# A two-layer diffusion block: first norm and projections in program order on three engines, the context's modulation sums queued behind the latents' steps, scalings on ScalarE

## The chip, the cores and the metric

The kernel runs on one core of one Trainium2 chip. The metric is the device time of one execution in microseconds (us). The core has five engines that work at the same time, each on its own queue of instructions in a fixed order: TensorE (PE, matmuls; PEld is its weight load), VectorE (DVE), ScalarE (ACT), GpSimd (POOL) and SyncE (SP, which here only issues DMA transfers; ACT issues a few too). Engines wait for one another through semaphores.

## The reference

512 latent tokens and 256 context tokens of width 1024 go through two layers. Cut to what matters:

```python
for l in range(2):
    sh1, sc1, gt1, sh2, sc2, gt2 = adaln(c, w_mod[l], b_mod[l])             # silu(c) @ w_mod + b_mod, six parts
    csh1, csc1, cgt1, csh2, csc2, cgt2 = adaln(c_ctx, w_mod[l], b_mod[l])   # the same for the context
    h_ctx = rms_norm(ctx, norm1[l]) * (1 + csc1) + csh1
    h = rms_norm(x, norm1[l]) * (1 + sc1) + sh1
    a_b, a_c, a_x, q, k, v, u, sv, g = split(h @ w_in[l])     # q and k: RMS norm per head, then rotary
    attn = softmax(q @ [k, k_ctx].T / 8) @ [v, v_ctx]         # latents see latents and context
    y_a = (a_b * conv3(a_c * a_x)) @ w_a                      # branch A
    y_b = attn @ w_b                                          # branch B
    y_c = (gelu(u) * (w_s @ rms_norm(gelu(sv)) + b_s)) @ w_c  # branch C
    x = x + gt1 * ((sigmoid(g_a) * y_a + sigmoid(g_b) * y_b + sigmoid(g_c) * y_c) @ w_o)
    x = x + gt2 * (silu(h2 @ w_ff1) * (h2 @ w_ff3)) @ w_ff2
    # in layer 0 the context goes through the same; in layer 1 only its keys and values are needed
```

## The kernel before

Everything is fp32, held transposed: channels on the 128 partitions in 8 blocks (KD), tokens along the row; columns 0 to 511 are latents (XS), 512 to 767 context (CS). A product in fp32 is made of three matmuls: each operand is split into a high part, rounded on ACT (L224), and a low part, the difference, on POOL or DVE (L225). `mm` runs high by high, high by low, low by high (L234). Weights arrive in pieces of 128x512 or 128x384 (`ws`, five buffers, L218) and become `wh` and `wl` (four buffers each).

The modulation is not a matmul: for each of the 8 blocks of a section (shift or scale) `mod_sums` loads a 128x1024 tile of w_mod (512 KB, L153) and makes one fused multiply and row sum on DVE (L156) with the activated condition, `sbc[:, 0]` for the latents and `sbc[:, 1]` for the context; `mod_rest` adds the bias and the norm's gain (L165, L168). `wm_stage` gives the tile one of three buffers.

The first layer starts so. x arrives in three transfers; `norm_stats` squares its blocks on ACT (L348, L351), adds them on DVE (L352), sums over partitions on PE (L355), takes the power -0.5 on POOL (L359) and spreads the result over a PSUM bank (RB, L365). Then, for block k = 0 to 7: two modulation sums (scale, then shift), `norm_apply` (y on DVE L374, shift on ACT L376 or L379, split into the pair h[k]; for odd k the low part is L377 on DVE, for even k L225 on POOL), and the six projections of this block (key, value, four queries), which gather in six PSUM banks over all k (`six`). `post_k`, `post_v` and `post_q` take them out: squares on ACT (L436), per-head sums on PE (L440), the gain (L477, L515) and rotary, for which ACT issues DMAs that swap rows (L530), splits (L491 to L494, L519 to L522). Branches A (`branch_a`, the convolution is L605 to L610) and C (`branch_c`, gelu L636, gain L655) project the latents' h again, ten projections with weights of two 256 KB pieces each. After that come the context's norm, keys, values and branch C, and attention.

The order on each queue is made by a planner: it goes through the written order and, by a timing model of its own, lets what is ready sooner go first. Written order gives only the priority. `ctx_mods` writes the context's sums in turns with the branches' steps; the context's norm is written behind them. A few transfers are held back by a one-column copy on POOL into their target (L553, L557, L563, L623).

## Time and profile before

| | us |
|---|---|
| median of 3 runs (1976.04 to 1977.44) | 1976.17 |
| profiled execution, its own time | 1975.22 |
| span of its profile | 1973.4 |
| PE busy | 1879.8 (95%) |
| DVE busy | 1164.6 (59%) |
| ACT busy | 747.8 (38%) |
| POOL busy | 859.9 (44%) |

Times in the profile count from the span's start. Busy shares are averages over the whole span, and stages differ. A row of windows gives, for one stretch, the busy time of each engine with its instructions in brackets, the clock that PE was granted as a share of its 2.4 GHz, the mean busy share of the DMA engines, and what they moved. A wait is put down to what ended it. An instruction's time holds what it waits for once it has started.

### The profile page before, as it was taken

How to read it: one execution, taken by the hardware profiler on the slowest of the kernel's cores; microseconds unless marked ns; L12 is line 12 of the kernel's file. 1: busy time of each engine (PE TensorE's matmuls, PEld its weight loads, DVE VectorE, ACT ScalarE, POOL GpSimd, SP SyncE). 2: the span in 40 equal slices, each digit the busy share in tenths (PEclk: the TensorE clock that was granted, in tenths of full speed). 3: DMA queues.
4: the chain of work that ended last, by engine and by line, in shares of the span. 5: the costliest groups of instructions: out<-in, count | busy, mean ns of one | idle time of the engine just before them, and what ended most of it. 6: DMA issues, size and time to landing. Idle time of an engine off the chain costs nothing.

```text
span 1973.4 us, 27588 instructions
## 1 busy us (share of the span) xinstructions
PE 1879.8 (95%) x10150; PEld 1654.6 (84%) x10150; DVE 1164.6 (59%) x1936; ACT 747.8 (38%) x1459; POOL 859.9 (44%) x722
## 2 busy tenths in 40 slices
PE   5789999999999899999999998999999999999999
PEld 3578998888889789899999987888888888888887
DVE  7877865535359887877676867549523362322222
ACT  4346765222223623232322345448533352313121
POOL 4678743534334415152433347854333253424232
PEclk9989999999999899999999998999999999999999
DMA  8933201324255142323323354410322433332311
GB/s 280 306 101 97 76 27 39 134 76 149 75 185 195 38 144 91 129 91 118 119 95 134 119 183 153 135 34 5 107 90 92 147 108 127 100 102 86 111 43 66
DMA packets 107735, 222.42 MB, mean 113 GB/s; under 512 B 12368, under 2 KB 19792, under 8 KB 107600
## 3 DMA queue, kind: packets, MB, share of 16 engines
q1 hardware_dynamic: 105536, 217.51, 33.0%
q10 hardware_dynamic: 2064, 3.15, 0.6%
q8 instruction: 80, 1.31, 0.3%
q14 instruction: 55, 0.45, 0.1%
HBM read 212.74 MB, written 5.24 MB: 110 GB/s over the span
## 4 chain that ended last, share of the span: by engine, by line
PE 73%; DVE 14%; issue 4%; ACT 3%; DMA 3%; POOL 2%; ACTq 0%; SPq 0%; DVEq 0%; POOLq 0%
PE wide L234 33%; PE pD L234 21%; PE pD L311 5%; PE wide L311 5%; PE pF L234 3%; DMA wm<-in_w_modT 2%; DVE wm L156 2%; PE pO L765 2%; DVE wl L225 2%; PE pPT L759 1%; PE wide L733 1%; DVE junk L156 1%; DVE nm L737 1%; DVE nacc L352 1%; DVE ptl L762 1%
## 5 line engine op out<-in xcount | busy, mean ns | idle before, releaser
L225 POOL TENSOR_TENSOR wl<-ws,wh 128x512 fp32r<-128x512 f32 (+2 forms) x338 | 484.4, 1445 | 462.5 <-ACT wh L224 376.0
L234 PE MATMUL wide<-A,wh 128*128 128x512 f32 (+2 forms) x1728 | 469.3, 367 | 17.4 <-ACT A L224 8.2
L234 PEld LDWEIGHTS wide<-A,wh 128*128 128x128 f32 x1728 | 302.8, 192 | 72.7 <-ACT A L224 10.2
L224 ACT CAST wh<-ws 128x512 fp32r<-128x512 f32 (+2 forms) x536 | 302.2, 607 | 65.4 <-issue 17.5
L234 PE MATMUL wide<-A,wl 128*128 128x512 f32 (+2 forms) x864 | 289.1, 366 | 4.9 <-POOL wl L225 4.9
L225 DVE TENSOR_TENSOR wl<-ws,wh 128x512 fp32r<-128x512 f32 (+1 forms) x198 | 168.4, 851 | 131.5 <-ACT wh L224 121.5
L234 PE MATMUL pD<-A,wh 128*128 128x512 f32 (+1 forms) x784 | 238.2, 384 | 6.6 <-ACT A L224 2.8
L156 DVE SCALAR_TENSOR_TENSOR wm<-wm,fixed 128x1024 f32<-128x1024 f32 x112 | 152.1, 1361 | 49.4 <-DMA wm<-in_w_modT 47.5
L234 PEld LDWEIGHTS wide<-A,wl 128*128 128x128 f32 x864 | 154.2, 192 | 30.7 <-POOL wl L225 6.3
L234 PEld LDWEIGHTS pD<-A,wh 128*128 128x128 f32 x784 | 147.3, 193 | 35.0 <-ACT A L224 3.2
L234 PE MATMUL wide<-u,wh 128*128 128x512 f32 (+1 forms) x600 | 149.5, 352 | 0.9 <-DVE xr L990 0.9
L234 PE MATMUL pD<-A,wl 128*128 128x512 f32 (+1 forms) x392 | 148.7, 382 | 0.0
L234 PE MATMUL pD<-u,wh 128*128 128x512 f32 (+1 forms) x456 | 118.2, 357 | 0.0
L234 PEld LDWEIGHTS wide<-u,wh 128*128 128x128 f32 x600 | 98.9, 188 | 17.3 <-DVE xr L990 1.2
L742 POOL TENSOR_SCALAR pp<-pp,nm 128x768 f32<-128x768 f32 (+1 forms) x80 | 66.8, 836 | 101.2 <-DVE nm L741 65.5
L225 POOL TENSOR_TENSOR u<-su,u 128x768 fp32r<-128x768 f32 (+1 forms) x44 | 72.4, 1655 | 85.2 <-ACT u L224 85.2
L803 ACT ACTIVATE gate<-wide 128x512 f32<-128x512 f32 (+1 forms) x56 | 26.7, 516 | 199.8 <-PE wide L234 199.2
L156 DVE SCALAR_TENSOR_TENSOR junk<-wm,fixed 128x1024 f32<-128x1024 f32 x48 | 68.2, 1420 | 54.3 <-DMA wm<-in_w_modT 47.2
L809 DVE SCALAR_TENSOR_TENSOR gate<-gate,pD 128x512 f32<-128x512 f32 (+1 forms) x45 | 25.6, 596 | 122.4 <-PE pD L234 99.8
L224 ACT CAST wh<-fw 128x512 fp32r<-128x512 f32 x80 | 48.5, 615 | 121.8 <-DVE fw L263 106.3
L224 ACT CAST u<-su 128x768 fp32r<-128x768 f32 (+1 forms) x44 | 31.7, 728 | 165.7 <-DVE su L885 93.9
L234 PE MATMUL wide<-u,wl 128*128 128x512 f32 (+1 forms) x300 | 89.4, 351 | 0.0
(248 smaller groups left out, 3827.0 us busy)
## 6 DMA issues: line engine op xcount, KB each, us to landing
ws<-in_w SPq DMA_DIRECT2D x252, 256.0 KB, 3.8
wm<-in_w_modT SPq DMA_DIRECT2D x112, 512.0 KB, 4.3
ws<-in_w_in SPq DMA_DIRECT2D x184, 256.0 KB, 2.9
ws<-in_w_o SPq DMA_DIRECT2D x48, 256.0 KB, 5.4
ws<-in_w_abc SPq DMA_DIRECT2D x32, 256.0 KB, 2.7
ws<-in_w_six SPq DMA_DIRECT2D x16, 192.0 KB, 4.5
xr<-in_xT SPq DMA_DIRECT2D x8, 384.0 KB, 7.6
ws<-in_w SPq DMA_DIRECT2D x16, 192.0 KB, 2.4
```

Of the source, the lines that this page charges most:

```text
L156: nc.vector.scalar_tensor_tensor(o, t, 1.0, sbc[:, c, :], op0=ALU.mult, op1=ALU.mult, accum_out=MOD[l][:, sec, b, c:c + 1])
L224: nc.scalar.copy(hi, src)
L225: (lo_eng or nc.gpsimd).tensor_tensor(lo, src, f(hi), op=ALU.subtract)
L234: nc.tensor.matmul(d[:, :b - a], lhsT=ww, rhs=aa[:, a:b], start=kk == 0 and i == 0, stop=kk == n - 1 and i == 2)
L311: nc.tensor.matmul(D, lhsT=x[:, kk * P:(kk + 1) * P], rhs=a, start=kk == 0 and i == 0, stop=kk == 3 and i == 2)
L352: nc.vector.tensor_tensor(acc[:, :n], acc[:, :n], sq[:, :n], op=ALU.add)
L733: nc.tensor.matmul(D[:, a - k0:b - k0], lhsT=q[:, c * P - q0:(c + 1) * P - q0], rhs=kt[:, a:b], start=i == 0, stop=i == 1)
L737: nc.vector.tensor_reduce(nm[:, 0:1], D[:, :nk], axis=AX.X, op=ALU.max, negate=True)
L742: nc.gpsimd.tensor_scalar(pt[:, :nk], pt[:, :nk], nm[:, 3:4], 0.0, op0=ALU.mult, op1=ALU.add)
L765: nc.tensor.matmul(o[:, 0:256], lhsT=v3[:, kt, :], rhs=pp[:, j * 256:(j + 1) * 256], start=gi == 0 and j == 0 and i == 0, stop=gi == len(k ...
L803: nc.scalar.activation(g_[:, a:e], D, AF.Tanh, scale=0.5)
L809: nc.vector.scalar_tensor_tensor(g_[:, a:e], g_[:, a:e], 1.0, D, op0=ALU.add, op1=ALU.mult)
```

## The change

The first norm and the six projections stand in a block in which DVE, POOL and ACT issue in the written order; PE and SP, and what is written outside the block, stay with the planner. The written order is new: the sums for block k + 1 stand around the step of block k (the scale's sum inside `norm_apply`, between y and the shift, the shift's sum behind it), and the weights of block k + 1 are split ahead of the matmuls of block k. The first scale sum stands between the squares' additions and the statistics. Latents' and context's first-section loads have a tag of their own, `wm0`, with five buffers. The Silu of the condition stands behind the squares, and a one-column Silu at the start loads its table.

The context's sums, and then its norm, are written step by step in turn with the branches (`ctx_norm`), each step within `later(...)`: what it issues on DVE (for the norm, on ACT too) comes in that engine's queue behind the latents' step marked last (`mark` on DVE, `amark` on ACT). That is an order of issue, not a wait for its end. Five kinds of scalings by a per-channel factor move from DVE (`tensor_scalar`) to ACT (`activation` with Copy and a scale): key, queries, the convolution's middle tap, the gain in branch C, for latents and context and in both layers. The context's x comes in one 1 MB transfer instead of eight, behind one copy.

```diff
-    def norm_stats(X, a, b):
+    def norm_stats(X, a, b, then=None):
...
+        if then:
+            then()
         st = pst("st")
...
         nc.vector.scalar_tensor_tensor(y, X[k][:, a:b], g, RB[:, :n], op0=ALU.mult, op1=ALU.mult)
+        if between:
+            between()
...
+    scr = sm.tile([P, 1], F32, tag="scr", name="scr", bufs=2)
+    nc.scalar.activation(scr, half[:, 0:1], AF.Silu)
...
-    nc.scalar.activation(sbc[:, 0, :], sbc[:, 0, :], AF.Silu)
+    mark, amark = [None], [None]
+
+    def later(ins):
+
+        return tc.issue_after(ins.ins)
...
-            nc.vector.tensor_scalar(kk[:, :n], D, vcol(l, V_KG), None, op0=ALU.mult)
+            nc.scalar.activation(kk[:, :n], D, AF.Copy, scale=vcol(l, V_KG))
...
-                nc.vector.tensor_scalar(qq[:, :n], D, vcol(l, V_QG), None, op0=ALU.mult)
+                nc.scalar.activation(qq[:, :n], D, AF.Copy, scale=vcol(l, V_QG))
...
-                nc.vector.tensor_tensor(qb[0:64, :n], qq[64:128, :n], f(qb[64:128, :n]), op=ALU.subtract)
+                mark[0] = nc.vector.tensor_tensor(qb[0:64, :n], qq[64:128, :n], f(qb[64:128, :n]), op=ALU.subtract)
...
-            RB = norm_stats(X, *XS)
-            for k in range(KD):
-                for sec in (1, 0):
-                    mod_sums(0, sec, k, (0,), wm_stage())
-                    mod_rest(0, sec, k, 1, 0, 1)
-                norm_apply(X, RB, G1[0], MOD[0][:, 0], k, *XS, h[k])
-                for hb in range(2):
-                    w = load_piece(w_six[k][:, hb * 384:(hb + 1) * 384])
-                    for b in range(3):
-                        mm([six[3 * hb + b]], w[b:b + 1], h, [XS], k=k)
...
-            for k in range(KD):
-                nc.gpsimd.tensor_copy(X[k][:, SEQ:SEQ + 1], f(h[4][0][:, 0:1]))
-                nc.sync.dma_start(X[k][:, SEQ:NT], xT[k][:, SEQ:NT])
+            def first_sums(k, secs):
+                if k < KD:
+                    for sec in secs:
+                        mod_sums(0, sec, k, (0,), wp.tile([P, 1024], F32, tag="wm0", name="wm0", bufs=5))
+                        mod_rest(0, sec, k, 1, 0, 1)
+
+            def six_weights(k):
+                return [p for hb in range(2) for p in load_piece(w_six[k][:, hb * 384:(hb + 1) * 384])]
+
+            with tc.manual_schedule(engines={mybir.EngineType.DVE, mybir.EngineType.Pool, mybir.EngineType.Activation}):
+                RB = norm_stats(X, *XS, lambda: (nc.scalar.activation(sbc[:, 0, :], sbc[:, 0, :], AF.Silu),
+                                                 first_sums(0, (1,))))
+                first_sums(0, (0,))
+                w = six_weights(0)
+                for k in range(KD):
+                    norm_apply(X, RB, G1[0], MOD[0][:, 0], k, *XS, h[k], lambda: first_sums(k + 1, (1,)))
+                    first_sums(k + 1, (0,))
+                    wk, w = w, six_weights(k + 1) if k < KD - 1 else None
+                    for b in range(6):
+                        mm([six[b]], wk[b:b + 1], h, [XS], k=k)
+                    if k == 0:
+                        nc.gpsimd.tensor_copy(sbc[:, 1, 0:1], f(h[0][0][:, 0:1]))
+                        nc.sync.dma_start(sbc[:, 1, :], conds[1:2, :].to_broadcast([P, 1024]))
+                    if k == 6:
+                        nc.scalar.activation(sbc[:, 1, :], sbc[:, 1, :], AF.Silu)
+            nc.gpsimd.tensor_copy(xin[:, :, SEQ:SEQ + 1], f(h[4][0][:, None, 0:1]).to_broadcast([P, KD, 1]))
+            nc.sync.dma_start(xin[:, :, SEQ:NT], xT[:, :, SEQ:NT].rearrange("k p t -> p k t"))
...
-                    nc.vector.tensor_scalar(cv[:, :n], z[:, :n], cw[1], None, op0=ALU.mult)
+                    nc.scalar.activation(cv[:, :n], z[:, :n], AF.Copy, scale=cw[1])
...
-                nc.vector.tensor_scalar(gs[t][:, :n], gs[t][:, :n], vcol(l, V_SG + t), None, op0=ALU.mult)
+                nc.scalar.activation(gs[t][:, :n], gs[t][:, :n], AF.Copy, scale=vcol(l, V_SG + t))
...
-            def ctx_mods():
+            def ctx_norm():
                 for k in range(KD):
-                    for sec in (1, 0):
-                        mod_sums(0, sec, k, (1,), wm_stage())
-                        if k == KD - 1:
-                            mod_rest(0, sec, 0, KD, 1, 1)
+                    with later(mark[0]):
+                        for sec in (1, 0):
+                            mod_sums(0, sec, k, (1,), wp.tile([P, 1024], F32, tag="wm0", name="wm0", bufs=5))
+                            if k == KD - 1:
+                                mod_rest(0, sec, 0, KD, 1, 1)
+                    yield
+                rest = norm(X, G1[0], MOD[0][:, 0], *CS, h)
+                go = True
+                while go:
+                    with later(mark[0]), later(amark[0]):
+                        go = next(rest, rest) is not rest
                     yield
...
-            run(ctx_mods(), small_x())
-            for _ in norm(X, G1[0], MOD[0][:, 0], *CS, h):
-                pass
+            run(small_x(), ctx_norm())
```

Left out of the diff here: `mark[0] =` or `amark[0] =` stands also before the convolution branch's copy (L595), its first product (L599) and its last (L610), before gelu (L636) and before the sum of branch C's squares (L646).

## Rows read from the trace of the kernel before

**Rows 1.** Windows of 100 us: length, PE, PEld, DVE, ACT, POOL (instructions), clock, DMA share, GB/s.
```profile
0.00:100.00 100.00, 62.39 (x259) 49.56 (x260) 80.38 (x132) 37.49 (x67) 56.80 (x51) 0.95 0.87 292
100.00:200.00 100.00, 90.54 (x528) 79.25 (x527) 73.25 (x121) 55.52 (x111) 74.75 (x60) 0.93 0.32 98
200.00:300.00 100.00, 98.72 (x719) 92.42 (x719) 79.31 (x157) 70.69 (x142) 59.42 (x56) 1.00 0.18 53
...
1200.00:1300.00 100.00, 99.98 (x504) 84.61 (x503) 56.33 (x78) 47.24 (x88) 75.84 (x55) 1.00 0.34 109
```

**Rows 2.** Windows cut at the stage's own events, the same columns.
```profile
27.00:64.00 37.00, 33.05 (x129) 25.28 (x130) 33.93 (x59) 16.41 (x34) 27.23 (x30) 1.00 0.86 289
64.00:90.00 26.00, 22.02 (x104) 18.13 (x103) 22.50 (x28) 8.74 (x16) 22.09 (x12) 0.99 0.88 299
90.00:107.00 17.00, 10.84 (x36) 8.55 (x36) 15.22 (x28) 2.79 (x5) 4.41 (x3) 0.61 0.73 231
107.00:142.00 35.00, 29.91 (x128) 24.15 (x129) 26.39 (x28) 16.54 (x29) 26.90 (x18) 0.90 0.27 83
142.00:166.00 24.00, 22.13 (x133) 19.95 (x131) 17.30 (x31) 11.20 (x24) 14.95 (x14) 0.93 0.26 81
```

**Rows 3.** PE's waits, 64 to 166 us: waiter, releaser, total, times, longest.
```profile
PE pKB L483 <- DVE v L507: 6.1, 1, 6.1
```

**Rows 4.** Instructions by line and shape, 64 to 166 or 0 to 166 us.
```profile
L156 DVE SCALAR_TENSOR_TENSOR wm<-wm,fixed 128x1024 f32<-128x1024 f32 x16 | 24.9, 1575 | 4.4 <-DMA wm<-in_w_modT 4.3
...
L352 DVE TENSOR_TENSOR nacc<-nacc,nsq 128x256 f32<-128x256 f32 x7 | 5.7, 807 | 0.5 <-ACT nsq L351 0.3
...
L655 DVE TENSOR_SCALAR gel<-gel,fixed 128x512 f32<-128x512 f32 x2 | 3.1, 1540 | 2.7 <-ACT gsq L644 2.7
...
L515 DVE TENSOR_SCALAR qq<-pD,fixed 128x512 f32<-128x512 f32 x2 | 1.5, 744 | 0.0
...
L436 ACT ACTIVATE hsq<-wide 128x512 f32<-128x512 f32 x3 | 1.8, 599 | 9.3 <-DMA sw<-kk 7.4 <-POOL wl L225 1.6 <-PE phst L440 0.3
```

**Rows 5.** Timeline of DVE, 57 to 170 us: start, duration, instruction.
```profile
63.04 0.75 DVE L377 SCALAR_TENSOR_TENSOR A<-ny,fixed,A 128x512 fp32r<-128x512 f32 x1
...
82.00 0.47 DVE L605 TENSOR_SCALAR acv<-az,fixed 128x512 f32<-128x512 f32 x1
...
102.10 1.23 DVE L156 SCALAR_TENSOR_TENSOR wm<-wm,fixed 128x1024 f32<-128x1024 f32 x1
...
126.44 1.35 DVE L605 TENSOR_SCALAR acv<-az,fixed 128x512 f32<-128x512 f32 x1
...
139.98 1.66 DVE L522 TENSOR_TENSOR qb<-qq,qb 64x512 fp32r<-64x512 f32 x1
...
163.86 0.63 DVE L377 SCALAR_TENSOR_TENSOR A<-ny,fixed,A 128x256 fp32r<-128x256 f32 x1
```

**Rows 6.** Timeline of all engines, 0 to 42 us.
```profile
17.36 1.22 DVE L156 SCALAR_TENSOR_TENSOR wm<-wm,fixed 128x1024 f32<-128x1024 f32 x1
...
24.88 1.40 DVE L374 SCALAR_TENSOR_TENSOR ny<-xin,fixed,pRB 128x512 f32<-128x512 f32 x2
```

**Rows 7.** Chain of work that ended last, 13 to 70 us: start, duration, what.
```profile
42.48 5.54 DMA wm<-in_w_modT
```

**Rows 8.** The DMA queue's own waits (SP), 60 to 170 us.
```profile
SPq L153 <- DVE wm L156: 11.7, 7, 2.7
```

**Rows 9.** Timelines of DVE and of POOL around 27 us.
```profile
26.27 1.21 DVE L156 SCALAR_TENSOR_TENSOR wm<-wm,fixed 128x1024 f32<-128x1024 f32 x1
...
27.41 2.28 DVE L156 SCALAR_TENSOR_TENSOR wm<-wm,fixed 128x1024 f32<-128x1024 f32 x1
...
27.10 1.51 POOL L225 TENSOR_TENSOR A<-ny,A 128x512 fp32r<-128x512 f32 x1 [3.24 <-ACT A L224]
```

**Rows 10.** POOL's instructions by line and shape, 64 to 166 us.
```profile
L225 POOL TENSOR_TENSOR wl<-ws,wh 128x512 fp32r<-128x512 f32 x26 | 42.5, 1648 | 4.6 <-ACT wh L224 4.4
...
L225 POOL TENSOR_TENSOR B<-mx,B 128x512 fp32r<-128x512 f32 x1 | 1.3, 1288 | 1.6 <-ACT B L224 1.6
```

More of the change, by code (lines that the diff above doesn't have):

```diff
@@ L366, in norm_stats, with norm_apply @@
         return RB
-    def norm_apply(X, RB, G, S, k, a, b, hk):
+    def norm_apply(X, RB, G, S, k, a, b, hk, between=None):
         n = b - a
@@ L553, in dit_block @@
-            nc.gpsimd.tensor_copy(sbc[:, 1, 0:1], f(h[0][0][:, 0:1]))
-            nc.sync.dma_start(sbc[:, 1, :], conds[1:2, :].to_broadcast([P, 1024]))
-            nc.scalar.activation(sbc[:, 1, :], sbc[:, 1, :], AF.Silu)
-            for k in range(KD):
-                nc.gpsimd.tensor_copy(X[k][:, SEQ:SEQ + 1], f(h[4][0][:, 0:1]))
-                nc.sync.dma_start(X[k][:, SEQ:NT], xT[k][:, SEQ:NT])
+            def first_sums(k, secs):
[3 more added lines that the diff above has]
+                        mod_rest(0, sec, k, 1, 0, 1)
@@ L594, in ev_ac @@
                     ACV["c"] = slot("ac", n)
-                    nc.scalar.copy(ACV["c"][:, :n], D)
+                    amark[0] = nc.scalar.copy(ACV["c"][:, :n], D)
                 def ev_ax(D, *_):
                     ACV["z"] = slot("az", n)
-                    nc.vector.tensor_tensor(ACV["z"][:, :n], ACV["c"][:, :n], D, op=ALU.mult)
+                    mark[0] = nc.vector.tensor_tensor(ACV["z"][:, :n], ACV["c"][:, :n], D, op=ALU.mult)
                 def ev_ab(D, *_):
@@ L609, in ev_ab @@
                                                    op0=ALU.mult, op1=ALU.add)
-                    nc.vector.tensor_tensor(cv[:, :n], cv[:, :n], D, op=ALU.mult)
+                    mark[0] = nc.vector.tensor_tensor(cv[:, :n], cv[:, :n], D, op=ALU.mult)
                     if ("a", t) not in br:
@@ L635, in go @@
                     g_ = slot("gel", n)
-                    nc.scalar.activation(g_[:, :n], D, AF.Gelu_apprx_tanh)
+                    amark[0] = nc.scalar.activation(g_[:, :n], D, AF.Gelu_apprx_tanh)
                     lst.append(g_)
@@ L645, in branch_c @@
             nc.scalar.activation(sq1[:, :n], gs[1][:, :n], AF.Square)
-            nc.vector.tensor_tensor(sq0[:, :n], sq0[:, :n], sq1[:, :n], op=ALU.add)
+            mark[0] = nc.vector.tensor_tensor(sq0[:, :n], sq0[:, :n], sq1[:, :n], op=ALU.add)
             st = pst("gst")
```

## The prediction

> **What bounds the kernel now.** I read windows of 100 us first: TensorE (PE) is busy 62.4 us of the first hundred, 90.5 of the second, 98.7 of the third and 99.98 of the hundred from 1200 us, where the second layer's projections run [rows 1]. So what can be won lies ahead of 200 us, and the reader is to see there a kernel that is not yet limited by PE. Windows cut at the stage's own events tell why [rows 2]. From 27 to 64 us (first norm, six projections) VectorE (DVE) is busy 33.9 of 37 us and the DMA engines 86%. From 64 to 90 DVE is busy 22.5 of 26 us, GpSimd (POOL) 22.1. From 90 to 107 DVE has 15.2 of 17 us, but PE 10.8 us at a mean granted clock of 0.61, and POOL 4.4: both wait for DVE. The longest PE wait in the stage says for what [rows 3]: 6.1 us ahead of the transposes for the keys (L483), until DVE had split the values (L507). From 107 to 142 and 142 to 166 DVE falls to 26.4 of 35 and 17.3 of 24 us.
>
> What filled DVE early? By line, 16 sums of L156 take 24.9 us between 64 and 166 us [rows 4]; they are the context's, and they are issued ahead of keys and queries that PE was waiting for. In DVE's timeline four events mark the stage [rows 5]: the last piece of the latents' h is made at 63.0 (done 63.8), the last of the context's sums starts at 102.1, the last query's low half ends at 139.98 + 1.66 = 141.6, and the context's norm ends at 163.86 + 0.63 = 164.5. Only then do context keys, context values and with them the scores have their input. I price the change by these dates: what the context's norm gains, the end gains, since behind it PE is busy 98.7 of 100 us [rows 1].
>
> **The start.** Between the squares and the statistics DVE did three sums (the last of them stands in [rows 6]), and the first normalized block came at 24.88 us. In the new order one sum stands there. Two sums of 1.22 us go: 2.4 us, the first block at about 22.5. The Silu that moves behind the squares, and the table load ahead of them, I cost at nothing: x arrives underneath. Without that cover it is one more step on ScalarE (ACT), below twice the 0.60 us of half as many columns [rows 4].
>
> **First norm to last h piece.** It takes 63.8 - 24.9 = 38.9 us now. In it the chain shows a wait of 5.54 us for one modulation load [rows 7]; and DVE adds the context's squares there (L352 at 256 columns, seven for 5.7 us [rows 4]). In the new order the context's norm is behind, five buffers instead of three take the loads, and SP's waits for them (11.7 us in seven, [rows 8], partly later) should shrink. What remains is DVE's own step: per block two sums, y and, every other time, a low half: 2 x 1.3 + 0.74 + 0.37 + 0.4 of small steps = 4.1 us, 33 us for eight. Against that stand in-order stalls on three engines: DVE, POOL and ACT can no longer step past a late load. So 0 to 6 us are won (6 is 38.9 - 33); I take 2.6, a little under the middle because of the stalls, and the last h piece ends at 63.8 - 2.4 - 2.6 = 58.8 us. The eight gated context loads become one behind one POOL copy; seven POOL copies go, under 1.1 us on an engine with gaps: nothing.
>
> **From h to the last query.** DVE's busy time from 64 to 142 is 22.5 + 15.2 + 26.4 = 64.1 us [rows 2]. The 16 sums (24.9 us) leave it. So do the scalings: key and four queries, each like the 744 ns row of L515, 3.7 us; two of L605, 1.8 us; the first of the two L655, 1.5 us [rows 4]. A part of the last two is waiting for POOL (L605 took 0.47 us at 82.0 and 1.35 at 126.4, [rows 5]), so I count 5.6, not 7. That leaves 33.6 us. How fully will DVE be busy without the sums as filler? The nearest row is 107 to 142 us, when no sum was left: 26.4 of 35, 75%. So 33.6 / 0.75 = 44.8 us, and the last query ends at 58.8 + 44.8 = 103.6 us; at full occupation 92. ACT gets nine scalings of about 0.60 us each (the 599 ns row of L436 reads the same shape, [rows 4]), 5.4 us in 102 us of which it works 39 or so: nothing, unless one of them stands in front of a cast for weights, and then 0.6 us each.
>
> **From the last query to the context's norm.** The first held sums stand behind the last query on DVE, later ones behind branch steps. Behind them on DVE queue the branches' products, and for these PE's banks wait. On SP a held sum keeps its buffer, so the sixth context load waits there, with weight pieces of the branches behind it; the price shown so far is 2.7 us for the longest such wait [rows 8]. DVE has then: its 17.3 us of 142 to 166 less 1.5 for the second L655, plus the sums, 24.9, plus the context's squares, 5.7: 46.4 us. With sums as filler DVE was busy 22.5 of 26 us (64 to 90), 87%: 53.3 us, the context's norm at 156.9. Ends: 150 at full occupation, 168 at the 72% of 142 to 166. Between these I choose the 87%, since then too sums and weight splits fill it, and lay 1.5 us of PE's recovered clock on top (10.8 us at 0.61 in [rows 2] is the largest such loss): 164.5 - 156.9 + 1.5 = 9 us.
>
> **Everything else.** The context's ten scalings and those of layer 1 leave DVE for ACT under PE's 98.7 and 99.98 us of 100 [rows 1]: nothing; without that cover 0.1 to 0.6 us each for some 19. Later work is planned anew with the same queues: plus or minus 2 us.
>
> The sum: the profiled execution took 1975.22 us; less 9 is 1966.2. The median of the runs shown is 0.95 above that execution, so **1967 us**. About 0.2%, 4 us, is what a measurement of this kernel can tell from no change.
>
> **A lock between DVE and POOL.** In [rows 9] a sum alone takes 1.21 us; the next starts at 27.41 while POOL splits from 27.10 to 28.61, and takes 2.28, ending 1.08 us after the split. The two did not overlap. The Trainium skill, SBUF — State Buffer, "Who interferes with whom", says that a DVE instruction with two SBUF inputs and a GpSimd instruction that reads SBUF exclude one another for their whole length; by that rule, which this row agrees with, reordering sums past splits gains no time in which both engines had work.
>
> **Rivals.** (1) DVE and POOL together are the bound. For it: from 64 to 90 us both show 85% and more, and 26 weight splits average 1648 ns where a lone split of that size takes 1288 [rows 2, 10]: each waits for the other. Then order changes nothing; only the earlier start (2.4 us) and the scalings of L605 taken off (1.8 us) remain: 4.2 us, **1972**. Against it: after 90 us POOL works 4.4 of 17 us and 15 of 24. (2) The other side: the last query comes late. Held sums need 53.3 us behind it, so from 164.5 - 53.3 = 111 us on the hold costs instead of gaining. Taking out sums gains nothing where DVE waited for the rotation's transfers, the transposes or POOL anyway; if half of 24.9 us comes back as waiting, the last query ends at 116, the context's norm at 169 to 174, say 9 us late: **1985**. For it: 25% idle from 107 to 142 with no sums about. Against it: at 90 to 107 PE waited for DVE itself. (3) PE becomes the bound: its idle time from 64 to 166 (4.0 + 6.2 + 5.1 + 1.9 = 17.2 us) and the clock lost there (10.8 x 0.39 + 29.9 x 0.10 + 22.1 x 0.07 = 8.7) both go, with the 5 of the start: 31 us, **1945**. For it: PE works 84.9 of these 102 us now, part of that below full clock [rows 2]. Against it: DVE's 46.4 + 33.6 us do not fit beneath that.
>
> **Chances and range.** The forecast (4 to 16 us won) 0.50; rival 1, 0.22, half of it over 4 us won; rival 2, 0.18, of it 0.15 beyond 4 us lost; rival 3, 0.10. So faster 0.50 + 0.11 + 0.10 = 0.71, same 0.14, slower 0.15. The range 1951 to 1979 leaves out most of rival 3 and of rival 2, some 0.19. The forecast's own range is 1959 to 1972.
>
> **What would show it.** In the new profile: first normalized block near 22.5 us; last h piece near 59; the last query's low half near 104, with all 16 context sums behind it; context's norm done near 157; PE above 12 us busy in the 17 us in which the keys are transposed, at a higher clock. If the last query comes later than 111 us, rival 2 holds; if sums behind it average over 2 us each, rival 1; if the last h piece is not before 62 us, my second term was wrong. A late weight piece on SP behind a held load would make the forecast wrong as well.

## The result, and the profile after

The changed kernel takes 1982.24 us (median of 7 runs, 1979.73 to 1985.29) against 1976.17 for the kernel before on the same chip (7 runs): 1.0031 times, 95% interval 1.0019 to 1.0042. It is slower by some 6 us, where 9 us of gain were forecast. Its profiled execution took 1980.03 us, 4.8 more than that of before.

Windows of 100 us of the changed kernel, to be read beside [rows 1]:

```profile
0.00:100.00 100.00, 70.15 (x292) 54.65 (x293) 69.27 (x107) 39.97 (x70) 53.03 (x48) 0.97 0.75 255
100.00:200.00 100.00, 79.31 (x452) 68.95 (x452) 75.81 (x121) 54.50 (x111) 72.19 (x51) 0.88 0.42 135
```

PE is busy 7.8 us more in the first hundred (62.4 before) and 11.2 less in the second (90.5 before). So something was won first and then more than lost. Cut at the events of the stage, the same columns:

```profile
27.00:62.00 35.00, 30.63 (x123) 22.71 (x122) 33.59 (x52) 14.04 (x25) 23.89 (x24) 1.00 0.98 337
62.00:90.00 28.00, 28.00 (x137) 23.43 (x136) 9.86 (x16) 9.88 (x19) 15.02 (x11) 1.00 0.47 157
90.00:120.00 30.00, 18.77 (x74) 14.08 (x73) 23.65 (x26) 11.97 (x20) 19.55 (x13) 0.79 0.42 136
120.00:145.00 25.00, 22.57 (x101) 18.11 (x99) 24.76 (x28) 14.09 (x25) 22.92 (x12) 0.98 0.62 196
145.00:170.00 25.00, 15.37 (x79) 13.88 (x80) 20.37 (x44) 10.78 (x24) 9.33 (x10) 0.66 0.18 54
```

Two lines matter. From 62 to 90 us PE is busy without a gap and DVE 9.9 of 28 us; before, DVE was busy 22.5 of 26 there and PE 22.0 [rows 2]. From 145 to 170 us PE has 15.4 of 25 us at a granted clock of 0.66 (the mean of stretches at 2.4 and at 1.2 GHz); before, 22.1 of 24 at 0.93. The timeline of DVE shows the events (start, duration, instruction, idle time before it and its releaser):

```profile
20.79 0.75 DVE L376 SCALAR_TENSOR_TENSOR ny<-xin,fixed,pRB 128x512 f32<-128x512 f32 x1
...
61.33 0.75 DVE L381 SCALAR_TENSOR_TENSOR A<-ny,fixed,A 128x512 fp32r<-128x512 f32 x1 [0.79 <-ACT A L380]
69.72 0.17 DVE L446 TENSOR_SCALAR hms<-phst 128x8 f32<-128x8 f32 x1 [7.64 <-PE phst L444]
...
78.09 0.69 DVE L620 TENSOR_TENSOR az<-ac,wide 128x512 f32<-128x512 f32 x1 [1.54 <-PE wide L234]
78.70 2.29 DVE L156 SCALAR_TENSOR_TENSOR wm<-wm,fixed 128x1024 f32<-128x1024 f32 x1
...
90.08 0.69 DVE L544 TENSOR_TENSOR kk<-rt,sw 128x512 f32<-128x512 f32 x1 [4.72 <-DMA ws<-in_w_in]
...
143.07 1.64 DVE L532 TENSOR_TENSOR qb<-qq,qb 64x512 fp32r<-64x512 f32 x1
144.73 1.23 DVE L156 SCALAR_TENSOR_TENSOR wm<-wm,fixed 128x1024 f32<-128x1024 f32 x1
...
168.90 0.88 DVE L381 SCALAR_TENSOR_TENSOR A<-ny,fixed,A 128x256 fp32r<-128x256 f32 x2
```

First normalized block at 20.8 us (24.9 before), last h piece done at 62.1 (63.8), first context sum only at 78.7 (64.8), last query's low half at 144.7 (141.6), context's norm at 169.8 (164.5) [rows 5, 6]. After the last h piece DVE stands for 7.64 us until PE has the head statistics, and then in pieces of 1.5 to 4.7 us: of the 27.9 us up to 90 it idles 18.1; in the kernel before it idled 3.5 of the 26.2 us between its last h piece and 90 (idle time is here, and below, a window's length less DVE's busy time in it). The first 14 sums do not come behind the queries but behind a branch step (L620 at 78.1), which the planner issues early, and they run among the queries' steps.

The date of the context's norm is DVE's work ahead of it plus DVE's idle time. One window up to that date, in the kernel before (DVE's busy time is the figure behind PE's and PEld's):

```profile
0.00:164.50 164.50, 119.42 (x525) 97.06 (x526) 129.48 (x202) 67.05 (x121) 100.17 (x83) 0.93 0.64 210
```

In the changed kernel:

```profile
0.00:169.80 169.80, 121.80 (x525) 96.98 (x526) 128.08 (x193) 71.39 (x130) 97.91 (x75) 0.91 0.61 206
```

The same of the kernel without the hold, e1 below:

```profile
0.00:155.50 155.50, 118.44 (x523) 94.55 (x524) 125.16 (x188) 71.28 (x129) 95.35 (x75) 0.95 0.67 225
```

And of the one with all sums behind the last query, e5 below:

```profile
0.00:166.70 166.70, 123.45 (x518) 98.49 (x519) 128.20 (x193) 71.09 (x130) 98.48 (x76) 0.90 0.60 205
```

The work hardly changes (129.5, 128.1, 125.2, 128.2 us). The idle time does: 35.0, 41.7, 30.3, 38.5 us. The 18 us that DVE waits ahead of 90 us are more than the difference between the changed kernel and e1 (11.4 us). They do not set the norm's date by themselves: e2, e4, e13 and e16 below, all with the hold, idle 17.0 to 18.0 us there too, but 31.9 to 36.1 us in all, and their norm is done at 159.5 to 164.5 us.

### The profile page after: what moved, and what is told of

It is laid out like the page before. It is cut to its first block, busy times and chain, and to the rows that moved or that the text cites. A ratio compares the mean times of both kernels' runs of the same rounds, so it can differ in the third digit from the quotient of the medians.

```text
span 1978.2 us, 27518 instructions
## 1 busy us (share of the span) xinstructions
PE 1879.9 (95%) x10150; PEld 1653.2 (84%) x10150; DVE 1148.2 (58%) x1908; ACT 760.9 (38%) x1487; POOL 856.0 (43%) x715
## 4 chain that ended last, share of the span: by engine, by line
PE 73%; DVE 14%; issue 5%; POOL 3%; DMA 2%; ACT 2%; ACTq 0%; DVEq 0%; SPq 0%; POOLq 0%
PE wide L234 33%; PE pD L234 20%; PE pD L311 5%; PE wide L311 5%; PE pF L234 4%; DVE wm L156 3%; PE pO L791 2%; PE pPT L785 2%; PE wide L759 2%; POOL wl L225 1%; DVE wl L225 1%; DVE junk L156 1%; DMA wm<-in_w_modT 1%; DVE xr L1016 1%; DVE nm L763 1%
## 5 line engine op out<-in xcount | busy, mean ns | idle before, releaser
L234 PEld LDWEIGHTS wide<-A,wh 128*128 128x128 f32 x1728 | 301.6, 191 | 79.2 <-ACT A L224 13.2
L224 ACT CAST wh<-ws 128x512 fp32r<-128x512 f32 (+2 forms) x536 | 301.8, 608 | 59.8 <-PE wide L234 11.2
L156 DVE SCALAR_TENSOR_TENSOR wm<-wm,fixed 128x1024 f32<-128x1024 f32 x112 | 156.3, 1400 | 46.3 <-DMA wm<-in_w_modT 44.5
L234 PEld LDWEIGHTS wide<-A,wl 128*128 128x128 f32 x864 | 153.2, 191 | 31.9 <-POOL wl L225 8.0
L234 PEld LDWEIGHTS pD<-A,wl 128*128 128x128 f32 x392 | 75.4, 192 | 19.9 <-POOL wl L225 6.2
```

The source lines that it names most:

```text
L156: nc.vector.scalar_tensor_tensor(o, t, 1.0, sbc[:, c, :], op0=ALU.mult, op1=ALU.mult, accum_out=MOD[l][:, sec, b, c:c + 1])
L224: nc.scalar.copy(hi, src)
L234: nc.tensor.matmul(d[:, :b - a], lhsT=ww, rhs=aa[:, a:b], start=kk == 0 and i == 0, stop=kk == n - 1 and i == 2)
```

## Experiments

In the expectations H stands for the hold: it takes the context's sums out of a stretch in which DVE otherwise waits. O is the written order on three engines, L the small one-column steps that wait for POOL's splits, S the scalings on ACT. Each kernel was timed against the kernel before on the same chip; before's medians in the four groups were 1976.48 (e1 to e4), 1975.98 (e5 to e8), 1976.52 (e9 to e12), 1976.27 (e13 to e16).

| run | median us | ratio to before | 95% |
|---|---|---|---|
| e8 the changed kernel again | 1979.97 | 1.0021 | 1.0013 to 1.0030 |
| e1 no hold | 1972.10 | 0.9976 | 0.9968 to 0.9985 |
| e5 all sums behind the last query | 1979.65 | 1.0021 | 1.0011 to 1.0032 |
| e6 before, hold alone added | 1981.01 | 1.0023 | 1.0013 to 1.0033 |
| e9 only the norm's steps held | 1965.71 | 0.9946 | 0.9934 to 0.9958 |
| e3 first stage free | 1976.98 | 1.0005 | 0.9996 to 1.0013 |
| e4 one-input small steps | 1976.04 | 0.9994 | 0.9986 to 1.0003 |
| e7 before, one-input small steps alone | 1977.16 | 1.0001 | 0.9992 to 1.0009 |
| e2 scalings back on DVE | 1978.11 | 1.0009 | 1.0000 to 1.0017 |
| e12 before, scalings on ACT alone | 1979.16 | 1.0010 | 1.0000 to 1.0020 |
| e10 no hold, one-input small steps | 1973.34 | 0.9987 | 0.9977 to 0.9997 |
| e11 no hold, free, one-input small steps | 1965.11 | 0.9939 | 0.9925 to 0.9954 |
| e16 e11 with the hold | 1971.25 | 0.9973 | 0.9963 to 0.9984 |
| e13 changed kernel, four buffers | 1978.31 | 1.0010 | 1.0001 to 1.0019 |
| e15 no hold, four buffers | 1970.69 | 0.9978 | 0.9968 to 0.9988 |
| e14 e11 with four buffers | 1968.04 | 0.9965 | 0.9952 to 0.9977 |

How far PE has come is worked out from the traces, which all hold 10150 matmuls: the start of matmul n, counted from 0, less that of matmul n in the kernel before, in us (minus is earlier). Each row is one execution; the two of the changed kernel (e8 is the second) differ by up to 1.7 us in these columns.

| n (its start before) | 300 (115) | 480 (157) | 960 (223) | 1400 (286) | 3300 (615) | 6300 (1167) | 6800 (1280) | last |
|---|---|---|---|---|---|---|---|---|
| changed | -12.8 | +5.2 | +7.4 | +6.0 | +5.9 | +3.2 | +4.8 | +4.9 |
| e8 | -12.4 | +6.9 | +9.1 | +7.7 | +7.7 | +4.6 | +6.2 | +4.9 |
| e1 | -11.6 | -7.0 | -4.9 | -3.5 | -3.7 | -4.4 | -2.1 | -2.9 |
| e5 | -14.2 | -1.0 | +6.5 | +7.4 | +6.5 | +6.9 | +7.2 | +7.0 |
| e6 | -19.9 | -1.1 | +5.7 | +3.9 | +1.2 | +1.1 | +8.3 | +6.4 |
| e2 | -19.4 | -0.1 | +0.7 | +0.5 | +0.2 | -2.7 | +4.0 | +3.7 |
| e12 | +4.4 | +2.1 | +3.4 | +2.7 | +0.6 | +1.7 | +6.9 | +6.8 |
| e9 | -16.1 | -7.6 | -6.4 | -6.1 | -12.6 | -13.3 | -10.8 | -12.3 |
| e11 | -4.9 | -6.1 | -4.9 | -5.7 | -7.4 | -9.2 | -7.3 | -8.8 |
| e16 | -19.0 | -4.3 | -2.2 | -3.3 | -3.3 | -4.5 | -2.4 | -3.3 |
| e3 | -14.8 | -2.4 | +2.2 | +2.4 | +2.2 | +2.3 | +5.4 | +4.1 |
| e4 | -19.7 | -5.0 | -3.2 | -3.0 | -2.9 | -2.8 | +1.6 | -0.3 |
| e10 | -9.2 | +0.9 | +4.8 | +4.0 | -1.5 | -2.2 | -0.1 | -0.1 |
| e13 | -20.8 | -0.9 | +1.8 | +2.1 | +1.9 | +1.4 | +5.7 | +5.5 |
| e15 | -9.8 | -7.3 | -6.8 | -6.1 | -6.2 | -5.8 | -3.3 | -5.5 |

**The hold taken off (e1).**

```diff
     def later(ins):
-        return tc.issue_after(ins.ins)
+        return ExitStack()
```

> The changed kernel with the holds alone taken out: the context's sums and norm are free for the planner again; the written order of the first stage and the scalings on ScalarE stay. Theory H (the hold costs: it takes 16 sums out of the stretch 62 to 90 us, where VectorE now idles 19 of 28 us, and puts them among the queries, where TensorE waits): VectorE idles under 6 us between the last h piece and 90 us, the last query's low half ends before 135 us instead of 144.7, the context's norm before 160 instead of 169.8, and the time is 1966 to 1974, 6 us or more under the changed kernel. Theory O (the written order of the first stage costs) and theory S (the scalings on ScalarE cost): no more than 2 us under the changed kernel, 1980 to 1984.

Measured: 1972.10 us. The context's sums run from 62.6 to 101.1 us at a mean of 1.58 us (1.76 with the hold), the last query ends at 132.9, the context's norm at 155.5. The same windows as above, of e1:

```profile
62.00:90.00 28.00, 24.83 (x101) 20.11 (x102) 25.29 (x36) 10.65 (x21) 17.07 (x11) 0.82 0.80 265
...
145.00:170.00 25.00, 23.30 (x183) 21.67 (x182) 19.69 (x34) 17.87 (x42) 18.81 (x16) 1.00 0.28 92
```

From 62 to 90 us PE starts 101 matmuls instead of 137 and DVE works 25.3 instead of 9.9 us; from 145 to 170 PE starts 183 instead of 79 at full clock. So with the hold PE runs ahead in the latents' branches, and then waits, in pieces, until the context's norm. What it is ahead by (12.8 us at the 300th matmul) is no gain, since e1 is 11.6 us ahead there too and keeps 7.0 at the 480th, where the changed kernel has lost 18.

Not all of the 18 us are a wait for DVE's work. PE's longest wait from 60 to 170 us in the changed kernel (total, times, longest) is for a split of weights on POOL, and on POOL this split stands behind a step of the rotation that waits for its transfers:

```profile
PE pD L234 <- POOL wl L225: 5.8, 1, 5.8
```

```profile
115.09 1.26 POOL L541 TENSOR_TENSOR sw<-sw,ropeS 128x512 f32<-128x512 f32 x1 [7.29 <-DMA sw<-qq]
```

The four transfers of this step, issued from 107.8 to 109.7 us, landed 4.8 to 5.5 us later, beside four loads for held sums (issued from 104.6 to 106.0) and two weight pieces; the four issued from 92.2 to 94.0, with no load under way, landed after 1.9 to 2.0. So held sums seem to cost by the place of their loads too; no run takes that apart from their place on DVE.

**All sums behind the last query (e5)**, which is how I had read the change.

```diff
+            qmark = mark[0]
             def ctx_norm():
...
-                    with later(mark[0]):
+                    with later(qmark):
                         for sec in (1, 0):
```

> The changed kernel with all 16 of the context's sums held behind the last query's low half on VectorE, as the prediction had supposed of the change, instead of each pair behind the step marked last. Theory H, which says that what counts is where sums stand among the queries: the last query's low half ends near 120 us or before instead of 144.7, but VectorE idles 25 us or more ahead of it, and the 16 sums with the context's squares and norm then take 45 to 53 us: context's norm at 165 to 173, time 1977 to 1985. The prediction's own reckoning gave: last query at 104, context's norm at 157, 1967.

Measured: 1979.65 us. The last query now ends at 119.6, all sums lie behind (119.7 to 153.4), the context's norm ends at 166.7, as H expected (DVE idles 23.3 us ahead of the last query, a little under the 25 expected). The two stretches, cut at the last h piece, the last query, the norm:

```profile
62.10:119.60 57.50, 53.77 (x250) 44.54 (x249) 34.16 (x39) 27.44 (x48) 42.35 (x28) 0.94 0.32 96
119.60:166.70 47.10, 32.36 (x130) 26.30 (x129) 44.32 (x73) 18.67 (x41) 24.89 (x17) 0.71 0.48 173
```

In the first DVE works 34.2 of 57.5 us while PE works 53.8: without the sums it is PE that sets the pace. In the second DVE works 44.3 of 47.1 and PE 32.4 at a clock of 0.71: DVE sets the pace. The hold puts DVE's work where PE needs DVE, and leaves DVE without work where PE is the bound.

**The hold alone, on the kernel before (e6), and the changed kernel again (e8).**

```diff
-            def ctx_mods():
+            def ctx_norm():
...
+                    with later(mark[0]):
...
-            run(ctx_mods(), small_x())
-            for _ in norm(X, G1[0], MOD[0][:, 0], *CS, h):
-                pass
+            run(small_x(), ctx_norm())
```

> The kernel before with the hold alone: the context's sums and norm in turns with the branches, each step behind the latents' step marked last; its own first stage, its scalings on VectorE and its three buffers for the loads stay. Theory H: VectorE idles 10 us or more between the last h piece and 90 us, the context's norm ends after 168 us instead of 164.5, the time is 1980 or more, 4 us or more over the kernel before. If the hold costs only together with the written order (a rival, theory O): within 2 us of the kernel before.

> The changed kernel itself, on the same chip and day as the experiments, nothing left out. All theories: 1979 to 1985, 1.0019 to 1.0042 times the kernel before; if it comes out within 2 us of the kernel before, what the first four runs won over it is partly a difference between chips.

Measured: e6 1981.01, e8 1979.97 us. The hold alone loses 5 us (1981.01 less 1975.98). But not where I had expected: the context's norm is done at 163.4 us, not behind 168. The first layer is 1.2 us behind at the 3300th matmul, and the rest arises between the 6300th and the 6800th, at the second layer's start (its first norm and projections), which the planner orders anew (from 1200 to 1300 us PE waits 3.1 us for weight splits, before not at all). DVE idles 13.2 us between the last h piece and 90 us, as H expected, but this did not make the norm late. So in e6 the time and the idle stretch bear H out, the norm's date does not.

**Only the norm's steps held (e9).**

```diff
-                    with later(mark[0]):
+                    with ExitStack():
                         for sec in (1, 0):
```
(and four buffers for `wm0`; five do not fit in this order)

> Only the hold on the context's 16 sums is taken off; the hold on the steps of the context's norm stays (the sums' loads have 4 buffers, since 5 don't fit in this order). Theory H (it is the sums, kept out of the stretch in which DVE otherwise waits): context sums within about 62 to 105 us, mean under 1.65 us, DVE idle between the last h piece and 90 us under 4 us (17.4 in the changed kernel), last query's low half before 138 us, and a median within 3 us of the 1972.1 us of the kernel with no hold at all. Rival (the hold on the norm's steps costs the time): context's norm done later than 165 us although the sums are early, and a median above 1977 us.

Measured: 1965.71 us, 6 less than the expected 1972 and so outside H's range too; sums from 61.2 to 108.2, DVE idle 3.8 us up to 90, last query at 136.3, norm at 159.8. With the norm's steps still held the loss is gone: it is the sums' hold that costs. Ahead of the 1400th matmul e9 stands 6.1 us ahead of before (e1 3.5). Of its further 6.5 us up to the 3300th, 4.8 have another reason, below under four buffers.

**The first stage left to the planner (e3).**

```diff
-            with tc.manual_schedule(engines={mybir.EngineType.DVE, mybir.EngineType.Pool, mybir.EngineType.Activation}):
+            with ExitStack():
```

> The changed kernel with the planner free to reorder VectorE, GpSimd and ScalarE in the first stage (the written order only as priority); holds and scalings stay. Theory O: first block to last h piece is 36 us or less instead of 41.3, and the time is 4 us or more under the changed kernel, 1978 or less. Theory H: the last h piece moves by 2 us at most either way, VectorE idles behind it as before, 1980 to 1985.

Measured: 1976.98 us. The first block is back at 24.5 us, but the last h piece is done at 57.6 instead of 62.1: the written order wins 3.7 us at the start and loses 8 in the eight blocks. These are O's numbers; H had expected 1980 or more. DVE still idles 14.7 us up to 90 (7.8 of it in one wait for PE's head statistics), and the norm ends at 162.1.

**The small steps with one input (e4), and this alone (e7).** The bias and gain come as per-partition scalars instead of second tensors.

```diff
+        if n * nc_ == 1:
+            m1 = MOD[l][:, sec, b0, c0:c0 + 1]
+            nc.vector.tensor_scalar(m1, m1, vcol(l, V_BM + sec * KD + b0), None, op0=ALU.add)
+            if sec == 1:
+                nc.vector.tensor_scalar(G1[l][:, b0, c0:c0 + 1], m1, 1.0, vcol(l, V_N1 + b0), op0=ALU.add, op1=ALU.mult)
+            return
```

> The changed kernel with the 24 one-column steps behind the latents' modulation sums written with the bias and the gain as per-partition scalars instead of second tensors (same numbers computed). Theory L (each such step waits for a GpSimd split because it reads two tensors: the one-column additions average 0.59 us here and 0.41 before where alone they take 0.15): they average under 0.25 us, first block to last h piece falls from 41.3 to 34 to 37 us, and with the hold still there the time falls by 3 to 6 us, to 1976 to 1979. Rival: one-column steps wait whatever they read (for the engine's order or a semaphore), and nothing moves by more than 2 us.

> The kernel before with the one-column steps' bias and gain as per-partition scalars, nothing else. Theory L: they average under 0.25 us instead of 0.37; the stage is bound there by loads and by stalls in order as much as by VectorE, so the last h piece moves from 63.8 to 60 to 63 us and the time by 0 to 4 us down, 1972.5 to 1976.5. Rival: nothing within 1 us either way, since VectorE's step is not the bound in the planner's order.

Measured: e4 1976.04, e7 1977.16 us. Lines of DVE up to the last h piece in the changed kernel (busy us, mean ns):

```profile
L165 DVE TENSOR_TENSOR fixed<-fixed 128x1 f32<-128x1 f32 x16 | 9.4, 588 | 0.6
...
L168 DVE SCALAR_TENSOR_TENSOR fixed<-fixed 128x1 f32<-128x1 f32 x8 | 4.9, 609 | 0.3
```

The same steps in e4:

```profile
L167 DVE TENSOR_SCALAR fixed<-fixed 128x1 f32<-128x1 f32 x16 | 3.4, 214 | 0.6
L169 DVE TENSOR_SCALAR fixed<-fixed 128x1 f32<-128x1 f32 x8 | 1.7, 214 | 0.3
```

14.3 us of one-column steps become 5.1, of which the 16 sums take back 2.4, and the last h piece is done at 57.9 instead of 62.1; step, stretch (37.2 us) and time are as L expected, within 0.2 us. In the kernel before, where the same steps took 8.7 us (411 and 291 ns on average), the new form brings nothing (1.0001): of the 3.7 us that the steps save, the 16 sums take back 1.4 (1.47 instead of 1.38 us on average), and the last h piece is not earlier (64.9 us), as the rival had it. I take it that the steps are dear where the written order lets nothing pass them; no run shows that by itself.

**The scalings back on DVE (e2), and on ACT alone (e12).**

```diff
-            nc.scalar.activation(kk[:, :n], D, AF.Copy, scale=vcol(l, V_KG))
+            nc.vector.tensor_scalar(kk[:, :n], D, vcol(l, V_KG), None, op0=ALU.mult)
```
(and so for the other four kinds; e12 has the opposite edit on the kernel before)

> The changed kernel with its five kinds of scalings back on VectorE; holds and written order stay. Theory S (scalings stand on ScalarE ahead of the casts for weights and behind the rotation's DMA issues, so weights come late): 4 us or more under the changed kernel, 1978 or less, and TensorE's 3.5 us wait for a cast near 94 us is gone. Theories H and O: VectorE gets 5 to 8 us of work back in the stretch behind the first stage, so the same as the changed kernel or up to 6 us over it, 1980 to 1988.

> The kernel before with only the five kinds of scalings moved to ACT. Theory S (they win in the second layer's projections, where PE waited for weight splits with the scalings on DVE, and cost something in the first): first layer 0 to 4 us behind the kernel before, second layer's projections the same as before, median 1974 to 1979 us. If they gain nothing and cost nothing anywhere: 1976 us within 1.5. If they are the reason for the slower result: above 1979 us.

Measured: e2 1978.11, 1.9 us below e8; e12 1979.16, 2.6 us above its before. On ACT the scalings win nothing and perhaps cost some 2 us. S's sign came in the first layer: from 60 to 170 us PE waits 12.0 us for casts and splits of weights in the changed kernel, and not at all in e2 (0.7 us in e1, so without the hold they are gone too); DVE's idle time up to the norm falls to 31.9 us, the norm comes at 164.5, and at the 1400th matmul e2 is 5.5 us ahead of the changed kernel. H and O, which had expected 1980 or more, were wrong there. In the kernel before, the scalings alone cost 2.7 us up to the same matmul (e12). S's other half falls: e12 loses 5 more at the second layer's start (1.7 to 6.9), where I had expected the scalings to help, and its median lies just above the 1979 that I had set for "they are the reason". But e2 loses 6.7 in the same place with the scalings on DVE. In that place every kernel of this study is later than before, by 0.3 to 7.2 us, among them e7 by 4.8, whose edit touches the first layer alone. So I take it for the planner's new order there and not for an effect of the scalings; no run takes it apart.

**Combinations (e10, e11, e16).** e10 is e1 with the small steps of e4 (four buffers); e11 is e1 with the edits of e3 and e4; e16 is e11 with the hold put back:

```diff
     def later(ins):
-        return ExitStack()
+        return tc.issue_after(ins.ins)
```

> No hold, and the one-column steps in the form with one input (4 buffers, since 5 don't fit). If the two losses are separate and add: last h piece near 60 us (64.5 without the hold alone), context's norm near 151 us, median near 1968 us. If they are two views of one stretch (DVE is full there once the sums are free, and what the small steps free is filled by sums): last h piece later than 62 us, context's norm 155 us or later, median 1971 to 1974 us.

> No hold, the first stage left to the planner, and the small steps with one input: of the change there remain the new written order, the five buffers of the sums' loads, the one context transfer and the scalings on ACT. If the order in three queues as written is of use by itself, this is slower than the kernel with the small steps and no hold, by 1 to 4 us: first normalized block near 24.5 us instead of 20.7. If the planner does as well: the same within 1.5 us, 1970 to 1974 us.

> The kernel of 1965.1 us with the hold put back, five buffers as there. Theory H: DVE idle between the last h piece and 90 us again above 10 us (1.0 without the hold), context's norm 4 us or more later than 158.3 us, median 1970 to 1977 us. If the hold costs only together with the written order of the first stage and the slow small steps: within 2 us of 1965.

Measured: e10 1973.34, e11 1965.11, e16 1971.25 us. e10 is as the second theory had it: the two losses do not add (last h piece 62.0, norm 162.3); without the shorter matmuls described below it would stand near 1978. e11 is the fastest version found, 0.9939 times before (0.9925 to 0.9954): first block at 24.3, last h piece at 55.4, context's sums 56.2 to 92.3, last query at 124.0, norm at 158.3. That the written order is of use by itself was wrong: without it e14 below, with four buffers as e10, is 5.3 us faster than e10. With the hold put back, DVE again idles 17.5 us up to 90 (3.6 without; 15.9 us of its waits from 60 to 170 are three for PE's head statistics, the longest 9.8, and 2.1 without), and 6.1 us are lost, as H expected; the norm is 3.0 us later (161.3), less than the 4 expected.

**Four buffers (e13, e14, e15).**

```diff
-                        mod_sums(0, sec, k, (0,), wp.tile([P, 1024], F32, tag="wm0", name="wm0", bufs=5))
+                        mod_sums(0, sec, k, (0,), wp.tile([P, 1024], F32, tag="wm0", name="wm0", bufs=4))
```
(and the same for the context's sums; e13 on the changed kernel, e14 on e11, e15 on e1)

> The changed kernel with four instead of five buffers for the sums' loads. If the shorter matmuls between 340 and 610 us come with four buffers: 512-column matmuls there at 391 ns, 4 to 6 us won in that stretch, median near 1975 us, the order ahead of 170 us as in the changed kernel (context's norm done at 167 to 172). If they come with the free order of the sums: 397 to 403 ns as before, median 1979 to 1983 us.

> The fastest kernel so far (no hold, first stage left to the planner, one-input small steps) with four buffers. If the shorter matmuls come with four buffers: 391 ns and 1960 us. If not: 1965 us within 2.

> No hold, four buffers. If the shorter matmuls come with four buffers and the hold of the norm's steps costs nothing: as the kernel with only the norm held, 1965.7 us within 2. If the hold of the norm's steps gained those 6 us: 1972 us, with 397 to 403 ns between 340 and 610 us.

Measured: 1978.31, 1968.04 and 1970.69 us. In e13 the norm is done at 163.6 us, ahead of the 167 to 172 that I expected, and its median lies between the two expected; e14 is 1 us outside its range. From 380 to 560 us, where the gates and the branches' output projections run behind attention, PE is without a gap in every kernel, but in e9 and e10 the matmuls are shorter (1040 start in these 180 us, in the others 1020 or 1021). A group of e9 by line and shape (busy us, mean ns):

```profile
L234 PE MATMUL wide<-A,wh 128*128 128x512 f32 x256 | 94.5, 391 | 0.0
```

The same group in e11:

```profile
L240 PE MATMUL wide<-A,wh 128*128 128x512 f32 x253 | 94.6, 397 | 0.0
```

From the 1800th to the 3300th matmul this is worth 4.8 us to e9 and 4.7 to e10. It does not come with four buffers (e13 to e15 move by 0.1 us or less there), nor with the free sums (e15), nor with the held norm steps (e10 has none). What sets it no run told. Without it e9 would stand near 1970.5, at e15's 1970.69: neither reason given for its lead was right (the 1972 expected of e15 came within 1.3 us), and the held norm steps neither win nor lose. e15 against e13 is one more pair for the hold: 7.6 us.

**The pairs together.** With and without the hold on the sums: e8 and e1 7.9 us, e13 and e15 7.6, e16 and e11 6.1, e6 and before 5.0; by the ratios to before, since some of these ran on different chips, 8.9, 6.3, 6.7 and 4.5. At the 3300th matmul these pairs lie 11.4, 8.1, 4.2 and 1.2 us apart, so in the first three the loss arises all or mostly up to there, in the last mostly later.

The fifth pair does not fit: e4 is only 2.7 us above e10, and e10 has the 4.7 us of shorter matmuls. Ahead of these, at the 1400th matmul, e10 without the hold (and with four buffers, where e4 has five) stands 6.9 us behind e4 with it: there the hold won. The hold does shorten the written first stage: from the first block to the last h piece it takes 41.3, 40.0 and 37.2 us with it (changed, e13, e4) and 43.9, 44.3 and 41.2 without (e1, e15, e10). Behind that stretch PE waits 11.2 us ahead of its head statistics in e10 (for three different steps), for causes that no run took apart.

Nor is the hold all that costs in the changed kernel. At the 3300th matmul e2, e3, e4 and e13, which keep the hold, are 5.7, 3.7, 8.9 and 4.0 us ahead of it (e1 9.6). They lose 3.2 to 6.7 us at the second layer's start (e1 2.3), and none of them ends clear of noise ahead of before, as e1, e9 and e15 do.

## Why the prediction was wrong, step by step

- **The start**: forecast 22.5, measured 20.8 us. The mechanism is right; the term was too small (4.1 us won, not 2.4). With the two sums went three of the five one-column steps there: they took 2.2 us ahead of the statistics, the two that are left 0.3.
- **First norm to last h piece**: forecast 36.3 us, measured 41.3. The mis-sized term is "0.4 of small steps": L165 twice and L168 once per block took 1.8 us (14.3 / 8). In program order no other step of DVE can run while one of them waits for POOL's split. With the one-input form the stretch took 57.9 - 20.7 = 37.2 us.
- **"The 16 sums leave" the stretch from h to the last query**: wrong as a reading of the change. `mark` is whatever step was written last, and the first 14 sums ran ahead of the last query's end, behind branch steps.
- **33.6 us of DVE work at 75% make 44.8**: the step that failed. e5 makes its assumption true and needs 57.5 us, with 34.2 us of DVE work: the work was right, the occupation is 59%. I took the 75% from 107 to 142 us, where branch steps filled DVE; the row of the stretch itself, 64 to 90 us [rows 2], shows PE busy 22.0 of 26 us: PE's gaps there, 4.0 us, were about all that taking sums out could win there. By [rows 2] PE works 62.8 us from 64 to 142, more than the whole 44.8, and in e5 still 53.8. The sums at 64 to 90 us ran under PE's projections and were nearly free. This is what I should have read.
- **53.3 us from the last query to the context's norm**: e5 measured 47.1, close to the 46.4 at full occupation. Together 104.6 us instead of 98.1, and the norm at 166.7 rather than 156.9: of these 9.8 us 6.5 are the two stretches, 3.3 the later h piece (62.1, not 58.8). With 47.1 for 53.3 the point from which the hold costs moves from 111 to 164.5 - 47.1 = 117.4 us, and e5's last query at 119.6 lies behind it, as its norm does behind 164.5.
- **1.5 us of recovered clock**: the wrong sign. PE ran ahead at full clock and then waited, and its clock was 0.66 from 145 to 170 us.
- **What the norm gains, the end gains**: not a rule. It fits the changed kernel's loss (5.3 us later, 4.8 us at the end), but in e13 and e6 the norm is 0.9 and 1.1 us earlier than before and the end 5.5 and 6.4 later, and e1's norm is 9.0 us earlier and its end 2.9, since 5 us are given back at the start of attention (it is 8.7 us ahead at the 540th matmul, 3.5 at the 1400th).
- **Scalings at nothing, later work within 2 us**: the scalings cost up to 2.6 us alone, and beside the hold 5.5 us up to the 1400th matmul (e2, where PE's 12.0 us of waits for weights are gone; the prediction priced a cast delayed by a scaling at 0.6 us); the second layer's new order moves single kernels by up to 7.2 us.
- **A late weight piece on SP behind a held load**: SP did stand 8.9 us before one held load (2.7 was the price shown), but PE waited only 1.1 us from 120 to 145. Its 5.8 us for weights ahead of that came from POOL's order, in which the split stood behind the rotation's transfers.
- **The rivals**: the second holds in its sign, with a smaller price (some 6 us, not 9), and its cause in part: DVE waits once the sums are gone, but longest for PE's head statistics, which it does not name, and most sums do not stand behind the last query. The first does not: the sums average 1.76 us, not over 2, and with the hold off the gain is there. What spoke for the second, idle DVE with no sums about, was in the text; I weighed against it PE's 6.1 us wait for one step, and held one wait to be the stretch.

## What to carry to other kernels

Work that is issued "too early" on a busy engine may be filler that runs in another engine's shadow: before moving it, read in the stretch it leaves which engine has no gap, and price the rest of the stretch by that one; and look at what its loads will then run beside. When an order is written out by hand, cost every small step by its time beside the neighbours it will then have, not by its shortest row. Undo each part by itself as well: here the rest of the change won 4 to 6 us without the hold on the sums (e1, e15; e9's 11 hold the 4.8 of unknown cause), and with it the whole lost 4 to 6. The parts do not add: the same hold won in one order of the rest (e4 against e10).

## What the runs showed of the hardware

A DVE step on one column with two inputs waited for POOL's splits. DVE's timeline in the changed kernel:

```profile
24.25 1.10 DVE L165 TENSOR_TENSOR fixed<-fixed 128x1 f32<-128x1 f32 x1
...
59.03 0.85 DVE L165 TENSOR_TENSOR fixed<-fixed 128x1 f32<-128x1 f32 x1
```

POOL's there:

```profile
56.83 3.04 POOL L225 TENSOR_TENSOR wl<-ws,wh 128x384 fp32r<-128x384 f32 x2
```

The step at 59.03 ends at 59.88, with POOL's splits at 59.87; at 20.70 us the same step takes 0.16. The Trainium skill, SBUF — State Buffer, "Who interferes with whom", says that a DVE instruction with two SBUF inputs and a GpSimd instruction that reads SBUF exclude one another for the instruction's whole length; this trace agrees, down to a single column. The form with a per-partition scalar took 0.21 us on average in the kernels that had it (e4, e7, e10, e11, e14, e16).

The same back-to-back 128x512 matmuls took 391 ns in two kernels and 395 to 403 in all others, by groups of the window from 380 to 560 us, at the same clock of 1.00 and with no wait between them.

The rotation's row swaps (`sw`) took longer beside large loads. Over all 18 traces, up to 170 us, they landed 2.3 us after issue on average when at issue no modulation load and no weight piece was under way (113 transfers, 1.9 to 4.3 us), and 4.5 us after when two modulation loads were and no weight piece (32 transfers, 2.0 to 7.5 us).
